# Token sums of a Strassen product on VectorE, three plain column blocks, earlier w_down loads, and an embedding gate without its ScalarE scaling

## The chip, the cores and the metric

The program runs on one core of a Trainium2 chip. The metric is the device time of one execution in microseconds (us), as a median of several executions. The engines' names in the profile are: PE is TensorE (matrix products and transposes), PEld its weight loads, DVE is VectorE, ACT is ScalarE, POOL is GpSimd, and SP is SyncE, which here only issues DMAs. L2209 means line 2209 of the kernel.

## What is computed

The program runs two transformer blocks over 1024 tokens of 1024 channels, all in fp32. The first block (two kinds of attention and a mixture of experts) and the mixer of the second are not touched. What matters is the end of the second block:

```python
h = rms_norm(x, g_ffn_pre[l])
up = h @ w_up[l]                                   # 1024 x 1024 by 1024 x 6144
gate_h = causal_dwconv(up[..., :D_FF], ffn_conv_w[l], ffn_conv_b[l])
hid = jax.nn.gelu(gate_h) * up[..., D_FF:]         # D_FF = 3072
x = x + rms_norm(hid @ w_down[l], g_ffn_post[l])

ple_gate = jax.nn.sigmoid(rms_norm(x, g_ple_gate[l]) @ w_ple_gate[l])
ple = rms_norm(p[l].astype(x.dtype) @ w_ple_proj[l], g_ple_post[l])
x = x + ple_gate * ple
```

## The kernel before

**Products.** Each fp32 operand is split into a high and a low half: the high half is a copy rounded by ScalarE (L86), the low half a subtraction on VectorE (L89; in some stages on POOL). A product is then three matmuls (L341 high by high, L342 low by high, L343 high by low). Tile names end in h and l: `wh`, `wl` are the halves of a weight chunk, `h3h`, `h3l` those of the normalized tokens of the FFN.

**Weight chunks.** A queue serves chunks in the order in which they are needed (`queue`, `pump`, `fetch`, `split_w`). A chunk takes a raw buffer, SP issues its DMA (L196), ACT and DVE split it into a pair of `wh`, `wl` slots, and the raw buffer is free again. A chunk's DMA can't be issued before a raw buffer is free, and SP issues in program order.

**The first FFN product, w_up.** There are `NC` = 24 column blocks, each with a gate half and a value half. The first `plain` = 2 blocks are computed directly: four chunks, each for two halves of 512 tokens, 24 matmuls for each half (192 in all). The order is half 0 of all four chunks first, then half 1, which needs the last token tile (tile 7). The other 22 blocks are Strassen pairs: gate and value chunk together take seven products of 12 matmuls (84 where the plain form takes 96). A pair has four weight parts: `u` and `v` are the loaded chunks, `s` and `d` are sums of them, made on POOL (`wsum`, L238) and split by ACT (L227) and DVE (L228). A block passes through a convolution gate (`fg`: ACT L2185, DVE L2188, gelu on ACT L2191), and DVE multiplies gate and value (L2209 in a plain block). The result is stored to DRAM (L2195) as `hid_d`.

**Token sums.** The Strassen products need sums of the tokens' quadrants, `t1` to `t4` (`fast_operands`, L262 to L304). They are made once, in two parts of 256 columns (`n` = 0, 1), while the plain blocks run. Each part is ten sums of 128x1024 (L272, L273): seven on POOL (`gp`), three on DVE (`dv`), chained through the temporaries `fty`, `ftx1`, `ftx3` and `ftx2`. Three splits give `ft1`, `ft2`, `ft3`; `t4` is split last, after the plain blocks.

Ahead of this stage the last token tiles are normalized: `max` sums on POOL (L2128), squares on ACT, a chain of tiny DVE steps (L401 to L411, tiles `nss`, `nr`, `ans`, `anr`), the scaled tile `nxn` (DVE, L2138), eight transposes on PE (L436, tile `tr`), and the split into `h3h`, `h3l`.

**The second FFN product, w_down** (`ffn_down`). Two halves of the tokens, each 24 steps over k with 24 matmuls, into all eight PSUM banks (tiles `tr`, `mm`). Chunks are the rows of w_down (`down`) and pairs of blocks of `hid_d` (`hid`); they are queued after `ffn_up` returns.

**The tail.** Eight token tiles, each with two column halves of 24 matmuls with `w_ple_gate`. The tokens' transposes `fhT`, `flT` come from `finish_pair`, two tiles at a time: norms, eight transposes of a tile, then ACT (L86) and DVE (L89) split them. Each half goes through a sigmoid (ACT L2416, tile `og`), a product with the embedding (DVE L2417), a sum (POOL L2418) and a DMA (L2419). The embedding `ple` of tile t + 2 is loaded after tile t (SP, L2398), scaled for each token by ACT (L2399) and multiplied by a gain on POOL (L2400); it has two buffers. In the tail ACT's instructions stand in the order in which the code writes them; elsewhere a scheduler orders each engine's instructions.

Of the kernel before, what the change touches and what calls it, by code (L numbers as in the profile page):

```python
# [17 lines left out]
F32 = mybir.dt.float32  # L18
# [49 lines left out]
class Kernel:  # L68
# [193 lines left out]
    def fast_operands(self, pool, tmp):  # L262
# [7 lines left out]
        dv, gp = nc.vector, nc.gpsimd  # L270
        f = lambda x: x.bitcast(F32)
        sub = lambda e, out, x, y: e.tensor_tensor(out, x, y, op=OP.subtract)  # L272
        add = lambda e, out, x, y: e.tensor_tensor(out, x, y, op=OP.add)  # L273
        x2s = [tmp.tile([P, 4, 256], F32, name=f"ftx2{n}") for n in range(2)]
        self.fast = dict(b11=b11, b21=b21, b22=b22, t1=t1, t2=t2, t3=t3, t4=t4)
        for n, x2 in enumerate(x2s):
# [3 lines left out]
            sub(gp, y, f(h12[1]), f(h11[1]))  # L280
            sub(dv, x1, f(h12[0]), f(h11[0]))
            yield 2.5
            add(dv, x1, x1, y)
            sub(gp, x3, f(h22[1]), f(h12[1]))
            yield 2.5
            self.split(*o1, x1)
            sub(gp, y, f(h22[0]), f(h12[0]))
            yield 2.5
            sub(dv, x2, f(h22[0]), x1)
            add(gp, x3, x3, y)  # L290
            yield 2.5
            add(gp, x2, x2, f(h22[1]))
            self.split(*o3, x3)
            yield 2.5
            self.split(*o2, x2)
            sub(gp, x2, f(h21[0]), x2)
            add(gp, x2, x2, f(h21[1]))
            yield 2.5

        def last():  # L300
            for n, x in enumerate(x2s):
                self.split(*(z[:, :, 256 * n:256 * n + 256] for z in t4), x)
# [1868 lines left out]
    def ffn_up(self, pu, up, pairs, es_t):  # L2171
# [55 lines left out]
        for c, (u, s, d, v) in enumerate(pairs, len(up) // 2):  # L2227
            add = lambda e, out, p, q: e.tensor_tensor(out, p, q, op=OP.add)  # L2228
# [40 lines left out]
    def block2(self, es):  # L2269
# [66 lines left out]
        NC, plain = DFF // P, 2  # L2336
# [24 lines left out]
        self.ffn_up(pu, up, pairs, es_t)  # L2361
        for half in range(2):
            for k in range(0, NC, 2):
                self.queue([hid[half][k // 2], *down[half][k:k + 2]])
        self.settle()
        es_u.close()
        es_h.close()
        acc = self.pool(es_x, "accp", side="right").tile([P, NT, D], F32, name="acc")
# [18 lines left out]
        self.add_w(es_x, "plew", 4, only=ch_p)  # L2387
# [5 lines left out]
        pl, embs = fin["pool"], []  # L2393

        def emb(t):
            if t < NT:
                e = pl.tile([P, D], F32, name="ple", tag="ple", bufs=2)
                nc.sync.dma_start(e, self.ple_d[t * P:(t + 1) * P])  # L2398
# [4 lines left out]
        with self.tc.manual_schedule(engines={mybir.EngineType.Activation}):  # L2403
            for t in range(2):
                emb(t)
# [169 lines left out]
```

## Time and profile before

| | |
|---|---|
| median of 3 executions | 3524.74 us (3518.86 to 3526.04) |
| the profiled execution | 3530.14 us, span 3528.4 us, mean granted clock of PE 0.952 |
| busy share of the span | PE 90%, PEld 72%, DVE 66%, ACT 45%, POOL 35% |
| PE, in tenths of 40 slices | `6987799788899799999888999999978999999997` |

The page gives shares of the span, and slices of 88 us each. A row of a timeline gives the start, the duration, the engine and line, what is written from what, and in brackets how long the engine had stood idle and what released it. Matmul durations overlap, since PE works on several at once, so the distance between two starts is what a matmul costs. A row of the windows gives for a stretch the busy time of every engine with the number of its instructions, PE's granted clock and the share of the DMA engines. The waits name the engine and line that stood idle, what it waited for, the sum, the number and the longest.

### The profile page before, as it was taken

To read this page: it belongs to the slowest core of one execution; us is meant where nothing else is said; L and a number is where in the kernel's file an instruction comes from. 1 tells how busy PE (TensorE), PEld (TensorE's weight loads), DVE (VectorE), ACT (ScalarE), POOL (GpSimd) and SP (SyncE) were. 2 spreads that over 40 slices of the span, in tenths; PEclk is the share of its full clock that TensorE was granted. 3 is DMA by queue.
4 is the path that set the end of the run, shared out by engine and by line. 5 is a ranking of instruction groups with operands and counts; after the bars stand their busy time and mean duration, and the time that the engine had idled before them with its cause. 6 is when DMAs were issued, how large, how long until landed. Compare 5 with 4: busy or idle time off the path is not lost. (4 is left out here: it accounts for less than half of the span.)

```text
span 3528.4 us, 40979 instructions
## 1 busy us (share of the span) xinstructions
PE 3170.0 (90%) x14117; PEld 2531.6 (72%) x14117; DVE 2314.9 (66%) x3549; ACT 1604.9 (45%) x2406; POOL 1247.4 (35%) x872
## 2 busy tenths in 40 slices
PE   6987799788899799999888999999978999999997
PEld 4865577567677577777666887888756877778776
DVE  6799954678655799999986554214477566653543
ACT  3553222568633566666566673211233333333332
POOL 2133223455204566666541121000136665520113
PEclk9998899889999799999999999999999999999998
DMA  5211366663454899999875213433341222244431
GB/s 192 62 51 55 109 220 200 152 167 80 150 172 154 300 320 317 316 320 325 292 239 162 67 56 107 135 115 109 119 128 60 82 80 78 78 173 143 163 112 60
DMA packets 365087, 548.42 MB, mean 155 GB/s; under 512 B 33292, under 2 KB 184224, under 8 KB 364876
## 3 DMA queue, kind: packets, MB, share of 16 engines
q1 hardware_dynamic: 343744, 503.53, 43.8%
q0 software_dynamic: 11440, 24.77, 2.7%
q10 hardware_dynamic: 9692, 17.48, 1.5%
q8 instruction: 112, 1.84, 0.2%
q14 instruction: 99, 0.81, 0.1%
HBM read 451.63 MB, written 88.78 MB: 153 GB/s over the span
## 5 line engine op out<-in xcount | busy, mean ns | idle before, releaser
L89 DVE TENSOR_TENSOR wl<-wr,wh 128x1024 fp32r<-128x1024 f32 (+1 forms) x489 | 821.2, 1703 | 473.9 <-ACT wh L86 472.9
L86 ACT ACTIVATE wh<-wr 128x1024 fp32r<-128x1024 f32 (+1 forms) x612 | 624.6, 1037 | 579.2 <-PE mm L342 179.5
L89 POOL TENSOR_TENSOR wl<-wr,wh 128x1024 fp32r<-128x1024 f32 x145 | 385.7, 2702 | 94.8 <-ACT wh L86 88.3
L341 PE MATMUL mm<-h2h,wh 128*128 128x512 f32 x576 | 229.4, 399 | 1.2 <-ACT h2h L86 1.2
L343 PE MATMUL mm<-h2h,wl 128*128 128x512 f32 x576 | 227.3, 395 | 0.0
L342 PE MATMUL mm<-h2l,wh 128*128 128x512 f32 x576 | 227.2, 394 | 0.0
L341 PE MATMUL mm<-wh,hTh 128*128 128x512 f32 (+1 forms) x368 | 145.1, 394 | 39.0 <-POOL wh L88 17.6
L343 PE MATMUL mm<-h3h,wl 128*128 128x512 f32 x416 | 165.2, 398 | 4.4 <-DVE ans L401 2.4
L341 PE MATMUL mm<-h3h,wh 128*128 128x512 f32 x416 | 167.4, 403 | 1.5 <-ACT wh L86 1.2
L342 PE MATMUL mm<-h3l,wh 128*128 128x512 f32 x416 | 165.2, 397 | 0.0
L2128 POOL TENSOR_TENSOR max<-max,antmp 128x512 f32<-128x512 f32 x16 | 25.2, 1600 | 386.3 <-DVE antmp L2127 374.5
L342 PE MATMUL pb<-wl,xgh 128*128 128x512 f32 x256 | 109.7, 429 | 48.5 <-DVE wl L89 47.3
L342 PE MATMUL mm<-wl,hTh 128*128 128x512 f32 (+1 forms) x368 | 142.3, 387 | 5.5 <-POOL wl L89 4.9
L343 PE MATMUL mm<-wh,hTl 128*128 128x512 f32 (+1 forms) x368 | 141.5, 385 | 0.0
L228 DVE TENSOR_TENSOR wl<-wsum,wh 128x1024 fp32r<-128x1024 f32 x44 | 55.4, 1259 | 119.4 <-ACT wh L227 119.4
L1384 POOL TENSOR_SCALAR sm<-sm,src 128x128 f32<-128x128 f32 (+7 forms) x128 | 96.2, 757 | 100.7 <-DVE src L1383 71.8
L341 PEld LDWEIGHTS mm<-h2h,wh 128*128 128x128 f32 x576 | 108.5, 188 | 27.5 <-ACT h2h L86 1.5
L342 PEld LDWEIGHTS mm<-h2l,wh 128*128 128x128 f32 x576 | 108.5, 188 | 26.2 <-issue 1.2
L343 PEld LDWEIGHTS mm<-h2h,wl 128*128 128x128 f32 x576 | 108.4, 188 | 25.2
L341 PE MATMUL mm<-hTh,wh 128*128 128x512 f32 x256 | 106.4, 416 | 19.6 <-POOL wh L88 12.1
L1409 DVE TENSOR_TENSOR ptl<-tr,pth 128x512 fp32r<-128x512 f32 x192 | 102.5, 550 | 26.0 <-ACT pth L1408 24.7
L342 PE MATMUL pa<-wl,xgh 128*128 128x512 f32 x256 | 103.4, 404 | 17.0 <-DVE wl L89 14.0
(667 smaller groups left out, 8909.5 us busy)
## 6 DMA issues: line engine op xcount, KB each, us to landing
wr<-in_exp_w SPq DMA_DIRECT2D x384, 512.0 KB
wr<-in_w_in SPq DMA_DIRECT2D x72, 512.0 KB
wr<-in_w_up SPq DMA_DIRECT2D x48, 512.0 KB
wr<-in_w_down SPq DMA_DIRECT2D x48, 512.0 KB
sg_d<-sg SPq DMA_DIRECT2D x64, 256.0 KB
score<-in_ada_w ACTq DMA_DIRECT2D x32, 512.0 KB
hid_d<-fg SPq DMA_DIRECT2D x24, 512.0 KB
wr<-hid_d SPq DMA_DIRECT2D x24, 512.0 KB
```

The lines of the kernel that those rows point to most:

```text
L86: self.nc.scalar.activation(hi, x, AF.Copy)
L89: (lo_eng or self.nc.vector).tensor_tensor(lo, x, hi.bitcast(F32), op=OP.subtract)
L228: nc.vector.tensor_tensor(lo, f, hi.bitcast(F32), op=OP.subtract)
L341: mm(ps, w[0], x[0], start=first, stop=False)
L342: mm(ps, w[0], x[1], start=False, stop=False)
L343: mm(ps, w[1], x[0], start=False, stop=last)
L1384: nc.gpsimd.tensor_scalar(sm, sm, rc[:, l:l + 1], 1.0, op0=OP.mult, op1=OP.mult)
L1409: self.lag.append(lambda c0=c0, th=th, tl=tl, tr=tr: nc.vector.tensor_tensor(tl[:, c0:], tr[:, c0:], th[:, c0:].bitcast(F32), op=OP.subtract))
L2128: nc.gpsimd.tensor_tensor(x[:, cs], x[:, cs], tmp, op=OP.add)
```

## The change

There are four parts.

- All twenty token sums are on DVE, in another order within a part, and part n = 1, which holds the last token tile, goes first.
- `plain` is 3: one block more is computed directly, and there is one Strassen pair fewer.
- The first six chunks of w_down's stage (`hid` 0, `down` 0, 1, `hid` 1, `down` 2, 3) are queued when the last but one Strassen pair begins (`near_end`), the rest after `ffn_up`; three more raw buffers (`ffz`) exist from then on.
- ACT no longer scales the embedding: the factor goes into DVE's product with `og`, which becomes a scalar_tensor_tensor. The embedding has three buffers, and the first three tiles are loaded and multiplied by the gain ahead of the second half of w_down; `w_ple_gate` gets three slots of its own instead of four.

```diff
--- before.py
+++ after.py
@@ -267,38 +267,38 @@
         b11, b21, b12, b22 = q(0, 0), q(1, 0), q(0, 1), q(1, 1)
         t = [tuple(pool.tile([P, 4, 512], F32R, name=f"ft{i}{x}") for x in "hl") for i in (1, 2, 3)] + [b12]
         t1, t2, t3, t4 = t
-        dv, gp = nc.vector, nc.gpsimd
         f = lambda x: x.bitcast(F32)
-        sub = lambda e, out, x, y: e.tensor_tensor(out, x, y, op=OP.subtract)
-        add = lambda e, out, x, y: e.tensor_tensor(out, x, y, op=OP.add)
-        x2s = [tmp.tile([P, 4, 256], F32, name=f"ftx2{n}") for n in range(2)]
+        sub = lambda out, x, y: nc.vector.tensor_tensor(out, x, y, op=OP.subtract)
+        add = lambda out, x, y: nc.vector.tensor_tensor(out, x, y, op=OP.add)
+        x2s = {n: tmp.tile([P, 4, 256], F32, name=f"ftx2{n}") for n in (1, 0)}
         self.fast = dict(b11=b11, b21=b21, b22=b22, t1=t1, t2=t2, t3=t3, t4=t4)
-        for n, x2 in enumerate(x2s):
+
+        for n, x2 in x2s.items():
             y, x1, x3 = (tmp.tile([P, 4, 256], F32, name=i, tag=i) for i in ("fty", "ftx1", "ftx3"))
             h11, h21, h12, h22, o1, o2, o3 = (tuple(z[:, :, 256 * n:256 * n + 256] for z in x)
                                               for x in (b11, b21, b12, b22, t1, t2, t3))
-            sub(gp, y, f(h12[1]), f(h11[1]))
-            sub(dv, x1, f(h12[0]), f(h11[0]))
+            sub(y, f(h12[1]), f(h11[1]))
+            sub(x1, f(h12[0]), f(h11[0]))
             yield 2.5
-            add(dv, x1, x1, y)
-            sub(gp, x3, f(h22[1]), f(h12[1]))
+            add(x1, x1, y)
+            self.split(*o1, x1)
             yield 2.5
-            self.split(*o1, x1)
-            sub(gp, y, f(h22[0]), f(h12[0]))
+            sub(y, f(h22[1]), f(h12[1]))
+            sub(x3, f(h22[0]), f(h12[0]))
             yield 2.5
-            sub(dv, x2, f(h22[0]), x1)
-            add(gp, x3, x3, y)
+            add(x3, x3, y)
+            sub(x2, f(h22[0]), x1)
             yield 2.5
-            add(gp, x2, x2, f(h22[1]))
             self.split(*o3, x3)
+            add(x2, x2, f(h22[1]))
             yield 2.5
             self.split(*o2, x2)
-            sub(gp, x2, f(h21[0]), x2)
-            add(gp, x2, x2, f(h21[1]))
+            sub(x2, f(h21[0]), x2)
             yield 2.5
+            add(x2, x2, f(h21[1]))
 
         def last():
-            for n, x in enumerate(x2s):
+            for n, x in x2s.items():
                 self.split(*(z[:, :, 256 * n:256 * n + 256] for z in t4), x)
 
         self.fast_last = last
@@ -2168,7 +2168,7 @@
         for i, ch in enumerate(chunks):
             self.dense_n(ch, src, lambda t, ps: emit(t, i % 2, ps), range(4 * (i // 2), 4 * (i // 2) + 4))
 
-    def ffn_up(self, pu, up, pairs, es_t):
+    def ffn_up(self, pu, up, pairs, es_t, near_end):
 
 
         nc = self.nc
@@ -2225,6 +2225,8 @@
             return ps
 
         for c, (u, s, d, v) in enumerate(pairs, len(up) // 2):
+            if c == NC - 2:
+                near_end()
             add = lambda e, out, p, q: e.tensor_tensor(out, p, q, op=OP.add)
             s1, s2, s3, s5 = (pu.tile([P, 512], F32, name=n, tag=n) for n in ("fs1", "fs2", "fs3", "fs5"))
             new(c)
@@ -2333,7 +2335,7 @@
         hp = self.pool(es_h, "hT3")
         self.hT, self.hcount = [hp.tile([P, KT, S], F32R, name=n) for n in ("h3h", "h3l")], 0
         wu, wd = a["w_up_2"][0], a["w_down_2"][0]
-        NC, plain = DFF // P, 2
+        NC, plain = DFF // P, 3
         self.hid_d = self.dram.tile([NC, P, S], F32, name="hid_d")
         blocks = [[blk(wu, i * DFF + c * P) for i in range(2)] for c in range(NC)]
         up = [self.chunk_t(b, KT) for x in blocks[:plain] for b in x]
@@ -2358,13 +2360,13 @@
         self.sums = pu = self.pool(es_u, "ffnu")
         self.later_steps(0.0, self.fast_operands(fp, self.pool(es_t, "fastt")))
         self.add_w(es_f, "ffx", 2, 2, side="right")
-        self.ffn_up(pu, up, pairs, es_t)
-        for half in range(2):
-            for k in range(0, NC, 2):
-                self.queue([hid[half][k // 2], *down[half][k:k + 2]])
+        later = [c for n in range(2) for k in range(0, NC, 2) for c in (hid[n][k // 2], *down[n][k:k + 2])]
+        self.ffn_up(pu, up, pairs, es_t, lambda: self.queue(later[:6]))
         self.settle()
         es_u.close()
         es_h.close()
+        self.add_w(es_x, "ffz", 0, 3, side="right")
+        self.queue(later[6:])
         acc = self.pool(es_x, "accp", side="right").tile([P, NT, D], F32, name="acc")
         self.hcount = 0
         ch_p = [Chunk([(lambda r: r, w.rearrange("(k p) c -> p k c", p=P))], [P, 2, 512])
@@ -2384,25 +2386,24 @@
                 next(fin[p], None)
 
         self.ffn_down(acc, hid[0], down[0], 0, lambda k, i: None)
-        self.add_w(es_x, "plew", 4, only=ch_p)
+        self.add_w(es_x, "plew", 3, only=ch_p)
+        pl, embs = fin["pool"], []
+
+        def emb(t):
+            if t < NT:
+                e = pl.tile([P, D], F32, name="ple", tag="ple", bufs=3)
+                nc.sync.dma_start(e, self.ple_d[t * P:(t + 1) * P])
+                nc.gpsimd.tensor_tensor(e, e, fin["ge"], op=OP.mult)
+                embs.append(e)
+
+        for t in range(3):
+            emb(t)
         self.queue(ch_p)
         todo = {(0, 7): [0], (2, 7): [0], (4, 7): [0, 1], (6, 7): [0, 1], (8, 7): [1],
                 (NC - 1, 4): [0], (NC - 1, 6): [0]}
         self.ffn_down(acc, hid[1], down[1], 1, lambda k, i: step(*todo.get((k, i), ())))
 
-        pl, embs = fin["pool"], []
-
-        def emb(t):
-            if t < NT:
-                e = pl.tile([P, D], F32, name="ple", tag="ple", bufs=2)
-                nc.sync.dma_start(e, self.ple_d[t * P:(t + 1) * P])
-                nc.scalar.activation(e, e, AF.Copy, scale=fin["r"][:, t:t + 1])
-                nc.gpsimd.tensor_tensor(e, e, fin["ge"], op=OP.mult)
-                embs.append(e)
-
         with self.tc.manual_schedule(engines={mybir.EngineType.Activation}):
-            for t in range(2):
-                emb(t)
             step(2)
             for t in range(NT):
                 x, e = fin["x", t], embs.pop(0)
@@ -2414,10 +2415,10 @@
                         self.mm3(ps, (x[0][:, k], x[1][:, k]), (wh[:, k % 2], wl[:, k % 2]), k == 0, k == KT - 1)
                     o = pl.tile([P, 512], F32, name="og", tag="og", bufs=2)
                     nc.scalar.activation(o, ps, AF.Sigmoid)
-                    nc.vector.tensor_tensor(o, o, e[:, cs], op=OP.mult)
+                    nc.vector.scalar_tensor_tensor(o, o, fin["r"][:, t:t + 1], e[:, cs], op0=OP.mult, op1=OP.mult)
                     (nc.vector if t == NT - 1 and c else nc.gpsimd).tensor_tensor(o, o, acc[:, t, cs], op=OP.add)
                     nc.sync.dma_start(self.out[0, t * P:(t + 1) * P, cs], o)
-                emb(t + 2)
+                emb(t + 3)
                 step(*{0: [1, 2], 1: [1, 1, 2], 2: [2, 3, 3], 3: [2, 2, 3], 4: [3], 5: [3, 3]}.get(t, ()))
         for c in ch_p:
             self.free(c)
```

On DVE at the end of the token norms, with token tile 7's split (`h3l<-tr,h3h`) and the sums (`fty`, `ftx`, `ft1l` to `ft3l`). Of before:

```order
L89 TENSOR_TENSOR wl<-wr,wh 128x1024
L402 TENSOR_SCALAR nr<-nss 128x1
L272 TENSOR_TENSOR ftx_21812<-h3h 128x1024
L403 TENSOR_SCALAR nr<-nr 128x1
L273 TENSOR_TENSOR ftx_21812<-ftx_21812,fty 128x1024
L407 TENSOR_SCALAR rst<-nr,nss 128x1
L407 TENSOR_SCALAR rst<-anr,ans 128x1
L411 SCALAR_TENSOR_TENSOR nr<-rst,nr 128x1
L272 TENSOR_TENSOR ftx_21809<-h3h,ftx_21812 128x1024
```

Here DVE's three sums of the first part stand between the tiny steps of the token norms (`nr`, `anr`). Of the change, from tile 7's scaled form on:

```order
L2138 SCALAR_TENSOR_TENSOR nxn<-max,nr,maf 128x1024
L2209 TENSOR_TENSOR fg<-mm,fg 128x512
L89 TENSOR_TENSOR h3l<-tr,h3h 128x4x128 x2
L271 TENSOR_TENSOR fty<-h3l 128x1024
L271 TENSOR_TENSOR ftx_21812<-h3h 128x1024
L271 TENSOR_TENSOR ftx_21813<-h3h 128x1024
L272 TENSOR_TENSOR ftx_21812<-ftx_21812,fty 128x1024
L271 TENSOR_TENSOR fty<-h3l 128x1024
L89 TENSOR_TENSOR ft1l<-ftx_21812,ft1h 128x4x256
```

No sum stands ahead of tile 7's split any more, and the first sum reads its `h3l`. Further on in the same run of rows, up to the weights of the third plain block:

```order
L89 TENSOR_TENSOR ft1l<-ftx_21919,ft1h 128x4x256
L272 TENSOR_TENSOR ftx_21920<-ftx_21920,fty 128x1024
L271 TENSOR_TENSOR ftx_21810<-h3h,ftx_21919 128x1024
L89 TENSOR_TENSOR wl<-wr,wh 128x1024
L2188 SCALAR_TENSOR_TENSOR fg<-fu_21798,colsc,fg 128x512
L89 TENSOR_TENSOR ft3l<-ftx_21920,ft3h 128x4x256
L2188 SCALAR_TENSOR_TENSOR fg<-fu_21798,colsc,fg 128x512
L272 TENSOR_TENSOR ftx_21810<-ftx_21810,h3l 128x1024
L89 TENSOR_TENSOR wl<-wr,wh 128x1024
```

Behind tile 7's split there are 21 sums and splits, and then, as the 22nd, the low half `wl` of the fifth plain chunk. The sixth chunk's `wl` is the 27th, the first pair's `u` the 30th. On POOL, the piece of the difference between the `max` sums of the token norms and the first pair's weight sums (the `x4` and `x2` rows of `max` become one row of eight):

```order
-L2128 TENSOR_TENSOR max<-max,antmp 128x512 x2
-L272 TENSOR_TENSOR fty<-h3l 128x1024
-L272 TENSOR_TENSOR ftx_21920<-h3l 128x1024
-L272 TENSOR_TENSOR ftx_21809<-h3h,ftx_21809 128x1024
-L273 TENSOR_TENSOR ftx_21809<-ftx_21809,h3l 128x1024
-L272 TENSOR_TENSOR fty<-h3h 128x1024
-L273 TENSOR_TENSOR ftx_21920<-ftx_21920,fty 128x1024
-L273 TENSOR_TENSOR ftx_21810<-ftx_21810,h3l 128x1024
-L272 TENSOR_TENSOR ftx_21810<-h3h,ftx_21810 128x1024
-L273 TENSOR_TENSOR ftx_21810<-ftx_21810,h3l 128x1024
```

POOL goes straight from the norms to the weight sums. On SP, the DMAs around the end of the Strassen pairs, before:

```order
L2195 DMA hid_d<-fg 128x1024
L196 DMA wr<-in_w_down 128x1024
L196 DMA wr<-hid_d 128x2x512
L2195 DMA hid_d<-fg 128x1024
L196 DMA wr<-hid_d 128x2x512
L196 DMA wr<-in_w_down 128x1024
L2195 DMA hid_d<-fg 128x1024
L196 DMA wr<-in_w_down 128x1024 x2
```

and of the change:

```order
L196 DMA wr<-in_w_up 128x8x128 x2
L2195 DMA hid_d<-fg 128x1024
L196 DMA wr<-hid_d 128x2x512
L196 DMA wr<-in_w_down 128x1024
L2195 DMA hid_d<-fg 128x1024
L196 DMA wr<-in_w_down 128x1024
L196 DMA wr<-hid_d 128x2x512
L196 DMA wr<-in_w_down 128x1024 x2
L2195 DMA hid_d<-fg 128x1024
```

Between the same three stores stood four chunks of w_down's stage, and now stand six, `hid` 0, `down` 0 and 1, `hid` 1, `down` 2 and 3, in the order in which they are used. On ACT in the tail, where a group of four `fhT` is the split of one tile's transposes, before:

```order
L2416 ACTIVATE og<-mm 128x512 x2
L2399 ACTIVATE ple<-ple,pler 128x1024
L86 ACTIVATE fhT<-tr 128x512 x4
L2437 ACTIVATE fj,fss<-acc 128x1024 x2
L2416 ACTIVATE og<-mm 128x512 x2
L2399 ACTIVATE ple<-ple,pler 128x1024
```

and of the change:

```order
L2417 ACTIVATE og<-mm 128x512 x4
L86 ACTIVATE fhT<-tr 128x512 x4
L2438 ACTIVATE fj,fss<-acc 128x1024 x2
L2417 ACTIVATE og<-mm 128x512 x2
L2438 ACTIVATE fj,fss<-acc 128x1024 x2
```

The split `fhT` stands directly behind the sigmoids; the scaling between them is gone.

## Rows read from the trace of the kernel before

**Rows 1.** Windows: stretch, its length, busy us (instructions) by engine, PE's clock, DMA, GB/s.

```profile
2595.00:2712.00 117.00, 82.82 (x334) 63.80 (x333) 100.01 (x127) 40.21 (x59) 75.94 (x38) 0.90 0.28 85
2712.00:3112.00 400.00, 399.95 (x1701) 317.38 (x1700) 244.97 (x285) 146.31 (x203) 235.39 (x160) 1.00 0.25 80
3121.00:3144.00 23.00, 18.38 (x67) 14.18 (x66) 11.43 (x21) 6.52 (x7) 3.40 (x3) 0.85 0.72 254
3395.00:3529.00 134.00, 104.59 (x459) 84.11 (x456) 50.79 (x91) 36.17 (x60) 46.38 (x25) 0.90 0.19 63
```

**Rows 2.** PE's timeline, from token tile 6's transposes to the second Strassen pair.

```profile
2638.31 1.94 PE L436 MATMUL tr<-ident,nxn 128*128 128x128 f32 x8 [10.71 <-DVE anr L411]
...
2648.75 0.80 PE L341 MATMUL mm<-h3h,wh 128*128 128x512 f32 x1 [0.25 <-ACT h3h L86]
...
2667.12 0.40 PE L341 MATMUL mm<-h3h,wh 128*128 128x512 f32 x1
2667.35 0.39 PE L342 MATMUL mm<-h3l,wh 128*128 128x512 f32 x1
...
2696.40 0.77 PE L341 MATMUL mm<-ft3h,wh 128*128 128x512 f32 x1 [8.12 <-DVE fg L2209]
...
2712.00 0.39 PE L341 MATMUL mm<-ft1h,wh 128*128 128x512 f32 x1
```

**Rows 3.** DVE's timeline over the token norms and the first sums.

```profile
2619.81 3.13 DVE L89 TENSOR_TENSOR wl<-wr,wh 128x1024 fp32r<-128x1024 f32 x1
...
2622.93 3.35 DVE L272 TENSOR_TENSOR ftx<-h3h 128x1024 f32<-128x1024 f32 x1
...
2626.39 2.13 DVE L273 TENSOR_TENSOR ftx<-ftx,fty 128x1024 f32<-128x1024 f32 x1
...
2628.81 2.21 DVE L411 SCALAR_TENSOR_TENSOR nr<-rst,nr 128x1 f32<-128x1 f32 x1
2630.94 1.21 DVE L272 TENSOR_TENSOR ftx<-h3h,ftx 128x1024 f32<-128x1024 f32 x1
...
2632.26 2.10 DVE L411 SCALAR_TENSOR_TENSOR anr<-rst,anr 128x1 f32<-128x1 f32 x1
2634.29 0.15 DVE L411 SCALAR_TENSOR_TENSOR nr<-rst,nr 128x1 f32<-128x1 f32 x1
...
2634.78 1.89 DVE L411 SCALAR_TENSOR_TENSOR anr<-rst,anr 128x1 f32<-128x1 f32 x1
...
2652.95 1.21 DVE L89 TENSOR_TENSOR ft3l<-ftx,ft3h 128x1024 fp32r<-128x1024 f32 x1
2654.09 1.21 DVE L89 TENSOR_TENSOR ft2l<-ftx,ft2h 128x1024 fp32r<-128x1024 f32 x1
```

**Rows 4.** POOL's timeline: a token sum, the first `d` sum of weights.

```profile
2660.98 3.26 POOL L273 TENSOR_TENSOR ftx<-ftx,h3l 128x1024 f32<-128x1024 f32 x1
...
2683.49 3.42 POOL L238 TENSOR_TENSOR wsum<-wr 128x512 f32<-128x512 f32 x2
```

**Rows 5.** PE's timeline at the start of w_down.

```profile
3121.36 0.39 PE L341 MATMUL tr<-wh 128*128 128x512 f32 x1
...
3137.50 1.65 PE L341 MATMUL tr<-wh 128*128 128x512 f32 x3 [4.11 <-ACT wh L86]
...
3139.37 0.63 PE L342 MATMUL tr<-wl,wh 128*128 128x512 f32 x1
3139.80 0.63 PE L343 MATMUL tr<-wh,wl 128*128 128x512 f32 x1
```

**Rows 6.** ACT's timeline at the start of w_down.

```profile
3136.39 2.00 ACT L86 ACTIVATE wh<-wr 128x1024 fp32r<-128x1024 f32 x2 [6.14 <-DMA wr<-in_w_down]
```

**Rows 7.** Waits of all engines in the tail: sum, number, longest.

```profile
ACT ple L2399 <- DMA ple<-ple_d: 36.1, 6, 9.4
...
PE mm L341 <- ACT fhT L86: 23.3, 3, 10.5
...
ACT og L2416 <- POOL og L2418: 6.7, 2, 4.4
```
## The prediction

> **What bounds the kernel now.** I read the page's slices first (PE at 7 or less in a few slices late in the program), then windows over the three places that the change touches, then the timelines there. In the Strassen pairs PE is full: 399.95 of 400 us, clock 1.00 [rows 1], so nothing can be won between 2712 and 3112 except by fewer matmuls. Three stretches are not full. From 2595 to 2712, where the token norms end, the plain blocks run and the sums are made, PE is busy 82.82 of 117 us. From 3121 to 3144, where w_down begins, it is busy 18.38 of 23. In the tail it is busy 104.59 of 134. In each the clock is below full (0.90, 0.85, 0.90). The gaps are 34.2, 4.6 and 29.4 us. A matmul costs 0.2325 us at full clock (2667.12 to 2667.35 in [rows 2]) and 0.43 at the lower level of 1.2 GHz (3139.37 to 3139.80 in [rows 5]).
>
> **A: the token sums and the third plain block.** PE's two long stalls are 10.71 us ahead of token tile 6's transposes and 8.12 us ahead of the first product on `ft3` [rows 2]. Both end on DVE. The reader is to see in [rows 3] why DVE is late: the same form of sum takes 3.35 us at 2622.93 and 1.21 at 2630.94, and a tiny L411 step takes 2.21, 2.10 and 1.89 where its like takes 0.15. The slow ones lie beside POOL's token sums, of which one takes 3.26 [rows 4].
>
> *Removed from the norm chain.* DVE's three sums between the tiny steps took 3.35 + 2.13 + 1.21 = 6.7 us; in the new order they stand behind tile 7. With POOL idle the three slow steps lose 6.20 - 0.45 = 5.8, and the `wl` at 2619.81 takes 1.21 in place of 3.13 (1.9). That is 14.4; I take 13.9, since hand-overs between engines stay. Tile 7's own chain holds no sum and keeps its length. So the first matmul of the second token half moves from 2648.75 [rows 2] to 2634.9.
>
> *Added behind it.* PE then has 96 matmuls on the four loaded chunks (22.3 us, to 2657.2), while DVE does tile 7's split and 21 sums and splits ahead of the fifth chunk's `wl`. Their pitch without POOL is 1.14 us (2652.95 to 2654.09 in [rows 3]): 23 x 1.14 = 26.2, so that `wl` ends at 2661.1. PE waits 2 to 4 us there, partly covered by matmuls that need only `wh`; with the slow clock behind it I take 3.6. The sixth chunk's `wl` comes five operations (6 us) later, under 10.7 us of matmuls on the fifth.
>
> *The weight sums.* In before the first `d` sum starts on POOL at 2683.49 [rows 4], because the token sums stand ahead of it. Now POOL has nothing else; the sum waits for the second raw chunk alone, and I place it near 2675, ahead of PE's use at about 2694. So the 8.12 us stall goes.
>
> *Sum.* From 2634.9: 96 + 96 plain matmuls (the third block included) and 84 of the first pair, 276 x 0.2325 = 64.2, plus 3.6, give 2702.7 for the start of the second pair, with four blocks done. In before the second pair starts 24 matmuls ahead of 2712.00 [rows 2], at 2706.4, with three blocks done; a pair takes (3121.36 - 2706.4) / 21 = 19.76 us [rows 2, 5], so four are done at 2726.2. The gain is 23.5; the third plain block's 12 extra matmuls (2.8 us) are inside it. I take 22, since one small stall I can't see is likely. Bounds: 12, if only the earlier tile 7 is won and a stall of some 10 us grows at the new `wl` waits; 26, if the fifth chunk is in time and the clock holds.
>
> **B: the start of w_down.** PE stops for 4.11 us at 3137.50 [rows 5], waiting for ACT's `wh`, which itself waited 6.14 us for a w_down chunk's DMA [rows 6]: the chunks pass one by one through a raw buffer. In the new order six chunks in order of use stand among the last stores, enough for 96 matmuls (22 us), and the extra buffers serve the next. The stall's 4.1 us go, and of the clock's loss in this window (0.15 of 23 us is 3.5 [rows 1]) the part that falls on matmuls, some 2.4: 6.5 together. Bounds: 0, if those buffers come no earlier than the old ones; 7.6, all of it. I am near the upper end because the waiting engine's row names the DMA, and the order moves just that. The small wait for a PSUM bank ahead of it stays.
>
> **C: inside w_down.** PE is the bound; three loads of `ple` and the POOL gain products beside it are hidden. Without POOL's cover the price would be a delayed `wl` of at most a sum's 3 us: bound 0 to 3 lost, taken at 0.
>
> **D: the tail.** The largest wait that PE meets is for `fhT` on ACT: 23.3 us in 3 times, the longest 10.5 [rows 7]. In the old order ACT's scaling of `ple` stands ahead of the split, and it waits 36.1 us in 6 times for its DMA, the longest 9.4. Take that away and ACT reaches the split right after the sigmoid. Two ACT instructions (36.17 / 60 = 0.6 us each [rows 1]) stay at each of the three transitions at most: between 0 and 3.6 us, so 19.7 to 23.3 are won; I take 21, and 1 more for matmuls that ran at the lower clock behind the three stalls (the window's clock of 0.90 would allow several). D is 22. What the scaling did moves into DVE's product; DVE is busy 50.79 of 134 us, so a slightly longer form costs nothing. What is late next is POOL: it now waits for the same DMA in its own queue, with the sums of `og` behind it, and SP's output DMAs behind those. But the tile loaded there is needed three tiles later, not two, and nobody on PE waits for an `og` sum until both `og` buffers are held. Bounds: 14, if a wait of POOL's kind returns in part; 27, with the clock.
>
> **Sum.** 22 + 6.5 + 22 = 50.5. The profiled execution took 3530.1 us, which would be 3479.6; it lay 5.4 above the median of the runs, so against the median I say **3474**. All three at their low ends (12 + 0 + 14 = 26) give 3499, all at their high ends (26 + 7.6 + 27 = 61) 3464; executions scatter by about 4 below.
>
> **Rivals.**
>
> *1. DVE becomes the bound of stretch A.* DVE is busy 100.01 of 117 us there, POOL 75.94 [rows 1]; fourteen sums more at 1.14 are 16 us, 116 of 117. If the 100 us were work that stays, the stretch could not become shorter, A would give nothing, and the time would be 3474 + 22 = 3496. Against it: much of the 100 us is not work, as the long and short rows of one form show (six rows of [rows 3] carry some 11 us of it). For it: the new sums all stand ahead of weights that PE wants. Chance 0.10. The Trainium skill's page Perfetto Trace Analysis, sections Identifying the Most-Contended Engine and Optimizing Scalar/DVE Operations, calls the engine with the highest occupancy the one to relieve, and advises handing work away from a saturated DVE, which speaks against this part; it adds that a move between GpSimd and DVE might not help, as they share a read port. By it the time is this rival's; the trace sides with the second half of the sentence more than the first, for the sums do slow each other.
>
> *2. POOL's wait takes ACT's place in the tail.* ACT already waits for POOL's `og` sums, 6.7 us in 2 times, the longest 4.4 [rows 7]. If such a wait stood ahead of each of the three splits, 3 x 4.4 = 13 us would return, less the 2 that I left there: 11, and 3485. For it: POOL works in order and its product now waits for the DMA. Against it: the third buffer. Chance 0.14.
>
> *3. The sums stay slow on DVE, and the weights queue behind them: slower.* If each of the 27 operations up to the sixth chunk's `wl` took the 3.35 us of the contended row instead of 1.14, they would end 90 us after 2634.9, at 2725; PE, with 96 matmuls and 46 of the fifth chunk (33 us) to do meanwhile, would stand some 57 us instead of my 3.6. That costs 54, as much as all three gains: 3474 + 54 = 3528. It decides from about 3.25 us an operation; below that the change is still faster. Against it: POOL has no sums left to contend with except weight sums that wait for raw chunks. Chance 0.04. The Trainium skill's page SBUF — State Buffer, section Who interferes with whom, states that a DVE instruction with two SBUF inputs contends with a GpSimd instruction that reads SBUF, and that the one shuts the other out for its whole length; by that only those few sums that meet one of POOL's are long, and the trace agrees so far, with 3.35 us beside POOL and 1.21 without.
>
> *4. The early queue does not load earlier.* If the six chunks find no free raw buffer until the last pair is done, B is 0: 3480.5. For it: the pair's two raw chunks hold buffers to its end. Against it: before, too, loads four chunks of this stage between the last stores. Chance 0.06.
>
> **How the numbers follow.** The forecast has 0.66. It and rivals 1, 2 and 4 lie between 3474 and 3496; with the bounds and the scatter of the terms I give 3460 to 3495, which leaves out rival 3, part of rival 1 and the forecast's own far ends, under 0.2 together. A measurement of this kernel tells about 0.2% (7 us) from no change. Faster by more than that: 0.95. Rival 3 lies at 3528 and spreads to both sides of 3532: within 0.2% 0.03, slower 0.02.
>
> **What would show it.** Right: no PE stall of 10 us at tile 6's transposes and none of 8 at the first `ft3` product; DVE's sums at about 1.2 us each; a short PE wait at the fifth plain chunk; 20 pairs that start near 2703; no wait for `wh` at the start of w_down; waits for `fhT` under 1.5 us each, in a tail of about 112 us instead of 134. Wrong: sums on DVE of 2 us and more, a new stall of PE at the plain chunks, PE waiting for `fhT` behind an `og` that waits for POOL, or a new stall in w_down beside POOL's gain products.

## The result and the profile after

The changed kernel takes 3471.48 us (median of 4, 3468.52 to 3474.49), the kernel before in the same comparison 3525.39 (3518.86 to 3528.51). The ratio is 0.9849, with a 95% interval of 0.9832 to 0.9867: 53.9 us faster. The forecast was 3474, between 3460 and 3495.

Ahead of the change the two programs are the same, and still their profiled executions differ there: token tile 4's transposes start at 2604.33 in before and at 2599.75 in after. So I count every stage from that point. From there to the last matmul before takes 918.3 us and after 863.3, 55.0 less. The page of after, its first part and PE's slices:

```profile
PE 3161.7 (91%) x14129; PEld 2522.5 (73%) x14129; DVE 2298.2 (66%) x3557; ACT 1595.0 (46%) x2396; POOL 1198.3 (35%) x850
...
PE   6997799788899789888888999999988999999998
```

The windows of after that answer to [rows 1]; the first is moved by the lead of some 4.6 us, the second lies within the pairs, the third and fourth begin as far ahead of their stage's first matmul as there:

```profile
2590.41:2707.41 117.00, 104.35 (x449) 81.80 (x448) 96.73 (x153) 47.91 (x68) 32.91 (x24) 0.99 0.33 99
2683.00:3083.00 400.00, 399.94 (x1698) 316.52 (x1698) 240.37 (x280) 144.79 (x199) 234.27 (x159) 1.00 0.25 82
3093.13:3116.13 23.00, 23.00 (x101) 18.45 (x100) 13.66 (x22) 6.80 (x8) 4.07 (x3) 1.00 0.84 296
3360.27:3468.90 108.63, 99.56 (x459) 80.05 (x456) 60.28 (x92) 30.64 (x55) 46.17 (x24) 0.99 0.23 73
```

In all three stretches the gap and the lower clock went together. In the first DVE did 14 sums more and was busy 96.73 us in place of 100.01. The start of w_down has no gap left. The tail is 25 us shorter with the same 459 matmuls.

PE's timeline of after, which answers to [rows 2, 5]:

```profile
2619.91 1.06 PE L436 MATMUL tr<-ident,nxn 128*128 128x128 f32 x8
...
2629.03 1.06 PE L436 MATMUL tr<-ident,nxn 128*128 128x128 f32 x8 [2.23 <-DVE nxn L2138]
...
2656.84 0.50 PE L343 MATMUL mm<-h3h,wl 128*128 128x512 f32 x1 [0.93 <-DVE wl L89]
...
2703.08 0.40 PE L341 MATMUL mm<-ft1h,wh 128*128 128x512 f32 x1
...
3093.49 0.40 PE L341 MATMUL tr<-wh 128*128 128x512 f32 x1
```

Tile 6's transposes start with no wait (before: 10.71), tile 7's wait 2.23 (before: 3.84), the fifth plain chunk's wait is 0.93, and no product on `ft3` waits. Every sum on DVE is now short (the source line of the first sums: engine, form, count, duration in ns as least, median, most):

```profile
L271 DVE TENSOR_TENSOR ftx<-h3h x4: 1218/1218/1220, 2632.7 to 2645.3; 128x1024 f32<-128x1024 f32 x4
```

and POOL comes to the first `d` sum of weights with idle time ahead of it:

```profile
2670.80 3.04 POOL L238 TENSOR_TENSOR wsum<-wr 128x512 f32<-128x512 f32 x2 [5.89 <-DVE wl L228]
```

By stages, from tile 4's transposes on (the difference of the first starts of each stage):

| stage | before | after | gain |
|---|---|---|---|
| A: to the first matmul of w_down | 517.0 | 493.7 | 23.3 |
| B, C: w_down, to the first matmul on `fhT` | 277.8 | 271.0 | 6.8 |
| D: the tail, to the last matmul | 123.4 | 98.6 | 24.8 |

In the tail no wait for `fhT` is left. The waits of PE and the longest of POOL for a DMA there:

```profile
PE tr L436 <- DVE flT L89: 3.5, 2, 2.8
...
POOL ple L2396 <- DMA ple<-ple_d: 15.1, 5, 4.2
```

### The profile page after: what moved, and what is told of

It reads as the page before. It is cut to its first block, busy times and chain, and to the rows that moved or that the text cites. A ratio compares the mean times of both kernels' runs of the same rounds, so it can differ in the third digit from the quotient of the medians.

```text
span 3468.9 us, 40965 instructions
## 1 busy us (share of the span) xinstructions
PE 3161.7 (91%) x14129; PEld 2522.5 (73%) x14129; DVE 2298.2 (66%) x3557; ACT 1595.0 (46%) x2396; POOL 1198.3 (35%) x850
## 5 line engine op out<-in xcount | busy, mean ns | idle before, releaser
L238 POOL TENSOR_TENSOR wsum<-wr 128x512 f32<-128x512 f32 x63 | 90.8, 1455 | 104.0 <-DVE wl L228 54.5
```

The source lines that it names most:

```text
L238: gp = lambda i, x, y, op: nc.gpsimd.tensor_tensor(f[:, i], x, y, op=op)
```

## The experiments

Eleven versions of the changed kernel; each diff is against it, and "..." stands for lines left out. A stage is read from one profiled execution of a version, a median from four to six executions, and the two can differ by up to 9 us. How far a stage scatters shows where versions run the same program in it: stage A took 493.4 to 495.6 us in nine traces, w_down 270.8 to 271.1 in four, the tail 98.0 to 100.8 in seven. So the stages and the waits in them decide, and the median is given beside them.

### The token sums back on POOL

All of `fast_operands` as before:

```diff
-        for n, x2 in x2s.items():
+        for n, x2 in enumerate(x2s):
...
-            sub(y, f(h12[1]), f(h11[1]))
-            sub(x1, f(h12[0]), f(h11[0]))
+            sub(gp, y, f(h12[1]), f(h11[1]))
+            sub(dv, x1, f(h12[0]), f(h11[0]))
...
```

> The changed kernel, with the token sums put back as they were: fourteen on POOL, six on DVE, part 0 first. The third plain block, the early queue and the tail stay. My theory: the gain of stretch A came from DVE no longer being slowed beside POOL ahead of tiles 6 and 7. Then DVE's sum of 3.3 us is back, PE stalls again for about 10 us at tile 6 and 4 at tile 7, and the time is 3471.5 + 13.8 + 1 = 3486 us. The 8 us stall at the first ft3 product should stay away, since the third plain block gives POOL 22 us more. Rival, the third plain block alone won stretch A: 3472.

Measured: 3488.73 us (ratio to before 0.9903, 0.9887 to 0.9920), and the stages are 17.1 us longer. PE waits again in the two old places (10.71 and 3.84 us in before), and for new reasons in the first pairs:

```profile
2629.27 1.94 PE L436 MATMUL tr<-ident,nxn 128*128 128x128 f32 x8 [7.37 <-DVE anr L411]
...
2638.46 1.94 PE L436 MATMUL tr<-ident,nxn 128*128 128x128 f32 x8 [3.40 <-DVE nxn L2138]
...
2713.85 0.50 PE L341 MATMUL mm<-ft1h,wh 128*128 128x512 f32 x1 [1.69 <-DVE fs L2230]
```

The second half of the tokens starts 13.4 us later than in the changed kernel, and the first pairs lose another 3.5 in three waits of 0.8 to 1.7. The 8 us stall did not return, so the third block does cover POOL, as expected. Next, this run's DVE rows:

```profile
2611.67 3.11 DVE L89 TENSOR_TENSOR wl<-wr,wh 128x1024 fp32r<-128x1024 f32 x1
...
2614.77 3.32 DVE L272 TENSOR_TENSOR ftx<-h3h 128x1024 f32<-128x1024 f32 x1
...
2619.70 2.28 DVE L411 SCALAR_TENSOR_TENSOR nr<-rst,nr 128x1 f32<-128x1 f32 x1
...
2623.04 0.26 DVE L407 TENSOR_SCALAR rst<-nr,nss 128x1 f32<-128x1 f32 x1
2623.22 2.10 DVE L411 SCALAR_TENSOR_TENSOR anr<-rst,anr 128x1 f32<-128x1 f32 x1
...
2625.73 1.89 DVE L411 SCALAR_TENSOR_TENSOR anr<-rst,anr 128x1 f32<-128x1 f32 x1
```

and POOL's at the same time:

```profile
2613.66 3.34 POOL L272 TENSOR_TENSOR ftx<-h3l 128x1024 f32<-128x1024 f32 x1
2619.56 2.40 POOL L272 TENSOR_TENSOR fty<-h3h 128x1024 f32<-128x1024 f32 x1 [2.56 <-DVE ftx L273]
2622.04 3.27 POOL L273 TENSOR_TENSOR ftx<-ftx,fty 128x1024 f32<-128x1024 f32 x1
2625.27 2.33 POOL L273 TENSOR_TENSOR ftx<-ftx,h3l 128x1024 f32<-128x1024 f32 x1
```

Add the durations. The three long L411 steps on one element per partition end at 2621.98, 2625.32 and 2627.62; POOL's sums end at 2621.96, 2625.31 and 2627.60. Each ends with POOL's instruction, as if it had stood still until then. DVE's sum at 2614.77 ends 1.1 us, its own length, after POOL's at 2617.00. The L407 step at 2623.04, which has one tensor input, takes 0.26 while POOL works. This is the rule that the prediction cited from the Trainium skill, SBUF — State Buffer, Who interferes with whom; this trace agrees, for the whole length of an instruction.

Not all of the 13.4 us is standing still. Up to tile 6 the rows of DVE beside POOL are 9.8 us longer than their likes (5.8 in the three L411 steps, 2.1 in the sum, 1.9 in a `wl` of 3.11 us). The rest is about what the three sums themselves take at 1.14 us each, which this version puts back ahead of tile 6. The order of the parts is tried alone further on.

### Two plain blocks

```diff
-        NC, plain = DFF // P, 3
+        NC, plain = DFF // P, 2
```

> The changed kernel with two plain blocks in place of three, so 12 matmuls less (2.8 us) and one Strassen pair more. My theory: the third block covers the sums on DVE; without it PE waits behind the sums at the first pair, for the s weights and the ft2 and ft3 operands, 3 to 9 us in all, so 3472 to 3478, most likely 3474. Rival, the cover is not needed: 3471.5 - 2.8 = 3468.7 or less.

Measured: 3474.91 (0.9863, 0.9846 to 0.9879); the stages are 7.7 us longer in its profile. The 2.8 us of matmuls that it saves are more than spent, above all by waits from the first pair's `u` on:

```profile
2646.95 0.61 PE L343 MATMUL mm<-h3h,wl 128*128 128x512 f32 x1 [2.42 <-DVE wl L89]
...
2661.46 0.50 PE L341 MATMUL mm<-ft3h,wh 128*128 128x512 f32 x1 [2.14 <-ACT wh L227]
...
2692.54 0.50 PE L341 MATMUL mm<-h3h,wh 128*128 128x512 f32 x1 [0.96 <-DVE fs L2230]
```

Seven such waits sum to 7.7 us. So the third plain block pays as cover for DVE's sums. Its median is only 3.4 us above that of the changed kernel, which the scatter can hide; the waits can't be argued away.

### Part 0 of the sums first

```diff
-        x2s = {n: tmp.tile([P, 4, 256], F32, name=f"ftx2{n}") for n in (1, 0)}
+        x2s = {n: tmp.tile([P, 4, 256], F32, name=f"ftx2{n}") for n in (0, 1)}
```

> The changed kernel with all sums on DVE, but part 0 first, which does not need token tile 7. The order then puts five sums of 1.14 us among the small steps ahead of tile 6's scaled form, and others ahead of tile 7's. My theory: both tiles are later by about 6 us, and the 0.9 us wait at the fifth chunk goes: 3477. Rival, with POOL quiet the order of the parts does not matter: 3471.

Measured: 3473.36 (0.9855, 0.9831 to 0.9880). Half of this was a miss. The lateness came: PE waits 10.35 us for tile 7's scaled form, and the second token half starts 7.2 us later than in the changed kernel.

```profile
2634.60 1.94 PE L436 MATMUL tr<-ident,nxn 128*128 128x128 f32 x8 [10.35 <-DVE nxn L2138]
```

But 3.9 us came back by the end of the pairs: 2.2 from more pairs at the quicker of two pitches (the last section says where these come from), the rest from the plain blocks, where PE no longer waits at the fifth chunk. The stages are 2.5 us longer, little more than their scatter; whether the order of the parts matters to the whole time stays open.

### No early queue and no extra buffers; each alone

```diff
-        self.ffn_up(pu, up, pairs, es_t, lambda: self.queue(later[:6]))
+        self.ffn_up(pu, up, pairs, es_t, lambda: None)
...
-        self.add_w(es_x, "ffz", 0, 3, side="right")
-        self.queue(later[6:])
+        self.queue(later)
```

> The changed kernel with all chunks of the w_down stage queued after the last Strassen pair again, and without the three extra raw buffers. My theory: the 4 us stall on ACT's wh early in w_down and the slow clock behind it are back: 3471.5 + 6.5 = 3478. Rival, the early queue loads nothing earlier: 3471.5, and the stall of before would be gone for another reason.

Only the buffers taken away:

```diff
-        self.add_w(es_x, "ffz", 0, 3, side="right")
```

> The changed kernel with the early queue of six chunks, but without the three extra raw buffers. My theory: the order in which the first six chunks take the buffers is what cures the start of w_down; PE is the bound after it, so the extra buffers give nothing: 3471 to 3473, and 271 us from the first matmul of w_down to the first on fhT, as in the changed kernel. Rival, the extra buffers do it: 279 us there and 3478.

Only the early queue taken away:

```diff
-        self.ffn_up(pu, up, pairs, es_t, lambda: self.queue(later[:6]))
+        self.ffn_up(pu, up, pairs, es_t, lambda: None)
...
-        self.queue(later[6:])
+        self.queue(later)
```

> The changed kernel with the three extra raw buffers, but with all chunks queued after the last pair. My theory: the first chunks still pass one by one through one early buffer, because the extra ones exist only once the last pair is done, so the stall of 4 to 5 us on ACT's wh comes back: 277 to 279 us from the first matmul of w_down to the first on fhT, 3477. Rival, the extra buffers do it: 271 us and 3472.

| | median us | ratio to before | w_down, to the first matmul on `fhT` |
|---|---|---|---|
| changed kernel | 3471.48 | 0.9849 (0.9832 to 0.9867) | 271.0 |
| neither | 3478.58 | 0.9870 (0.9854 to 0.9887) | 279.4 |
| early queue alone | 3467.40 | 0.9838 (0.9824 to 0.9852) | 270.8 |
| extra buffers alone | 3472.22 | 0.9851 (0.9834 to 0.9868) | 276.7 |

PE's waits at the start of w_down with neither (rows of its timeline):

```profile
3109.00 1.65 PE L341 MATMUL tr<-wh 128*128 128x512 f32 x3 [4.70 <-ACT wh L86]
...
3122.96 0.50 PE L341 MATMUL tr<-wh 128*128 128x512 f32 x1 [1.35 <-ACT wh L86]
```

and the one with the extra buffers alone:

```profile
3109.64 1.65 PE L341 MATMUL tr<-wh 128*128 128x512 f32 x3 [4.76 <-ACT wh L86]
```

The early queue does it, the buffers spare at most the second, smaller wait and are worth nothing beside the queue. The waits show this, the medians don't: the median with the extra buffers alone, 3472.22, is where I had put the rival, though its profiled execution, the one with the stall, took 3477.18. The median of the early queue alone lies below the 3471 to 3473 that I expected, and the intervals of the two ratios overlap.

The reason differs a little from what I had written. The late queue loads as many chunks early. Of the version with neither, first SP's issues, then ACT's splits:

```profile
3048.37 0.37 SPq L196 DMA_DIRECT2D wr<-hid_d  x1
3056.37 0.35 SPq L196 DMA_DIRECT2D wr<-in_w_down  x1
3068.21 0.33 SPq L196 DMA_DIRECT2D wr<-in_w_down  x1
3075.29 0.37 SPq L196 DMA_DIRECT2D wr<-hid_d  x1
3084.04 7.30 SPq L196 DMA_DIRECT2D wr<-in_w_down  x2
...
3081.49 1.05 ACT L86 ACTIVATE wh<-wr 128x1024 fp32r<-128x1024 f32 x1
3088.66 1.06 ACT L86 ACTIVATE wh<-wr 128x1024 fp32r<-128x1024 f32 x1 [2.53 <-DMA wr<-in_w_down]
3094.17 1.06 ACT L86 ACTIVATE wh<-wr 128x1024 fp32r<-128x1024 f32 x1 [4.46 <-DMA wr<-in_w_down]
```

Four chunks are on their way by 3075.29, as in the changed kernel by 3077.22, but ACT splits one and must then wait for two w_down chunks that SP issues only from 3084.04 on. In the changed kernel its splits up to 3096.01 wait for no load. So the early buffers went to chunks that are not the first in use (which ones, the traces don't name), and what the early queue mends is who gets the early buffers.

### The tail: scaling and buffers apart

The tail of before (scaling on ACT, two buffers, the loads of the first two tiles at the start of the tail):

```diff
-        for t in range(3):
-            emb(t)
...
-                e = pl.tile([P, D], F32, name="ple", tag="ple", bufs=3)
+                e = pl.tile([P, D], F32, name="ple", tag="ple", bufs=2)
...
+                nc.scalar.activation(e, e, AF.Copy, scale=fin["r"][:, t:t + 1])
...
+            for t in range(2):
+                emb(t)
...
-                    nc.vector.scalar_tensor_tensor(o, o, fin["r"][:, t:t + 1], e[:, cs], op0=OP.mult, op1=OP.mult)
+                    nc.vector.tensor_tensor(o, o, e[:, cs], op=OP.mult)
...
-                emb(t + 3)
+                emb(t + 2)
```

> The changed kernel with the tail of before: ACT scales the embedding, two buffers, the loads of the first two tiles in the tail. My theory: three waits of PE for fhT, some 23 us in all, are back, and the clock's loss behind them: the stretch from the first matmul on fhT to the last, 98.6 us in the changed kernel, becomes about 123, and the time 3471.5 + 24 = 3495. Rival, the wait only changes its place: 3472 to 3483.

Scaling on ACT, but three buffers and early loads:

```diff
+                nc.scalar.activation(e, e, AF.Copy, scale=fin["r"][:, t:t + 1])
                 nc.gpsimd.tensor_tensor(e, e, fin["ge"], op=OP.mult)
...
-                    nc.vector.scalar_tensor_tensor(o, o, fin["r"][:, t:t + 1], e[:, cs], op0=OP.mult, op1=OP.mult)
+                    nc.vector.tensor_tensor(o, o, e[:, cs], op=OP.mult)
```

> The changed kernel with ACT's scaling put back, but with the three buffers and the early loads kept. My theory: what counts is that ACT, in its fixed order, waits for a DMA that SP can issue only behind the tile's output; the third buffer doesn't change that. So the waits for fhT are back as in the kernel with the whole tail put back: 3491 to 3495. Rival, the third buffer and the early loads are what cured it: 3472 to 3475.

No scaling on ACT, two buffers and no early loads:

```diff
-        for t in range(3):
-            emb(t)
...
-                e = pl.tile([P, D], F32, name="ple", tag="ple", bufs=3)
+                e = pl.tile([P, D], F32, name="ple", tag="ple", bufs=2)
...
+            for t in range(2):
+                emb(t)
...
-                emb(t + 3)
+                emb(t + 2)
```

> The changed kernel without ACT's scaling, but with two buffers and the loads in the tail as before. My theory: POOL waits for the DMA off PE's path, so the gain is there without the third buffer: 3471 to 3474. Rival, POOL's late gain product holds the sums and the og buffers, and ACT's sigmoids stand ahead of fhT: 3480 to 3490.

| scaling on ACT | buffers, first loads | median us | ratio to before | tail us |
|---|---|---|---|---|
| no | 3, early | 3471.48 | 0.9849 (0.9832 to 0.9867) | 98.6 |
| no | 2, in the tail | 3468.75 | 0.9848 (0.9830 to 0.9866) | 99.4 |
| yes | 3, early | 3487.21 | 0.9896 (0.9880 to 0.9911) | 119.2 |
| yes | 2, in the tail | 3495.60 | 0.9920 (0.9904 to 0.9936) | 125.9 |

By the tails the scaling on ACT costs 26.5 us with two buffers and 20.6 with three. By the medians it is 26.9 and 15.7; the profiled execution with scaling and three buffers took 3496.84, the longest of its six. The third buffer and the early loads (not tried apart) give nothing without the scaling. With it they spare one of three waits, since one load of six comes early: a gain of 6.7 us in the tail where I had expected none, and a median below the 3491 to 3495 that I had put down. The waits of the tail with scaling and three buffers (with two, PE waits 26.0 us in 3 times):

```profile
ACT ple L2396 <- DMA ple<-ple_d: 34.5, 5, 9.7
...
PE mm L341 <- ACT fhT L86: 19.4, 2, 10.7
```

Without scaling and with two buffers POOL waits for that DMA instead, and PE has no wait for `fhT`:

```profile
POOL ple L2401 <- DMA ple<-ple_d: 16.3, 5, 4.7
```

### The residual sums of the tail on DVE

After the change PE's only waits in the tail are for `flT`, 3.5 us in 2 times. DVE's rows of the changed kernel ahead of the longer one show two `og` products that take 5.63 us:

```profile
3410.65 5.63 DVE L2418 SCALAR_TENSOR_TENSOR og<-og,pler,ple 128x512 f32<-128x512 f32 x2
3416.20 1.87 DVE L89 TENSOR_TENSOR flT<-tr,fhT 128x512 fp32r<-128x512 f32 x3
```

and POOL's rows show its two residual sums at the same time, as with the token sums:

```profile
3409.66 6.07 POOL L2451 TENSOR_TENSOR acc<-acc,fx 128x1024 f32<-128x1024 f32 x2 [1.21 <-issue]
```

```diff
-            nc.gpsimd.tensor_tensor(acc[:, t], acc[:, t], xt[j], op=OP.add)
+            nc.vector.tensor_tensor(acc[:, t], acc[:, t], xt[j], op=OP.add)
```

> The changed kernel with the residual sum of the last norms (acc + fx, eight of 128x1024, about 3.05 us each on POOL) on DVE. The one PE wait of the tail that is left, 2.8 us for flT at 3416.9, stands behind two og products that take 5.6 us beside those sums. My theory: the sums take 1.2 us each on DVE, the products 0.7 again, the wait goes, and the tail is 2 to 4 us shorter: 3468 to 3470. Rival, DVE has no room there and flT waits behind the sums: 3471.5 or more.

Measured: 3464.16 (0.9830, 0.9812 to 0.9849). The tail takes 96.3 us, and w_down 268.8 in place of 271.0, where a 1.86 us wait for a `wl` beside such a sum is gone too. By the stages this is 4 us, the upper end of what I had expected; the median lies 7.3 us below the changed kernel's, more than the traces explain. DVE does sums and products in less time than the products alone took:

```profile
3411.43 2.35 DVE L2451 TENSOR_TENSOR acc<-acc,fx 128x1024 f32<-128x1024 f32 x2
3413.70 1.41 DVE L2418 SCALAR_TENSOR_TENSOR og<-og,pler,ple 128x512 f32<-128x512 f32 x2
```

### Residual sums on DVE and no extra buffers

```diff
-        self.add_w(es_x, "ffz", 0, 3, side="right")
...
-            nc.gpsimd.tensor_tensor(acc[:, t], acc[:, t], xt[j], op=OP.add)
+            nc.vector.tensor_tensor(acc[:, t], acc[:, t], xt[j], op=OP.add)
```

> The changed kernel without the three extra raw buffers and with the residual sums of the last norms on DVE: the two edits of earlier runs together. If they add up, the stretch from token tile 4's transposes to the last matmul is 859 us, where the changed kernel has 863, with the tail at 96 in place of 98.6 and the 1.9 us wait inside w_down gone; the time 3464 to 3468. Rival, DVE is now too full in the tail and the og products or flT come late: 3470 or more.

Measured: 3463.78 (0.9823, 0.9810 to 0.9837); 858.8 us from tile 4's transposes to the last matmul, against 863.3. By the stages it beats both kernels. By the median it is 7.7 us below the changed kernel's, though they were timed in different comparisons.

## Why the prediction was right

**A, 22 forecast, 23.3 measured.** The first matmul of the second token half came 13.8 us earlier (18.4 less the 4.6 of lead), where the chain gave 13.9; putting the sums back cost 13.4 there. DVE's pitch of 1.14 us held. The first `d` sum came where it was expected (2670.80 and the lead make 2675.4, against 2675), though its row waits for DVE's `wl` of the part before it and not for a raw chunk.

At the fifth chunk the forecast had 3.6 us, for a wait and the slow clock behind it. The trace has a wait of 0.93 and full clock behind it, but that is the chance of this execution. Of nine versions traced that run the same program here, four wait 0.93 to 0.99 us and five 2.40 to 2.42. The one with neither early queue nor extra buffers waits 2.41. Windows from the first matmul of the second half to the end of that wait, and the 5 us behind it, of the changed kernel and then of that version:

```profile
2630.34:2656.84 26.50, 25.57 (x102) 20.21 (x102) 26.47 (x25) 10.89 (x13) 0.00 (x0) 0.94 0.00 1
2656.84:2661.84 5.00, 5.00 (x21) 4.06 (x22) 5.00 (x6) 1.70 (x2) 1.04 (x1) 1.00 0.37 105
...
2628.32:2654.75 26.43, 24.02 (x103) 19.12 (x103) 26.39 (x25) 11.00 (x13) 0.00 (x0) 1.00 0.00 1
2654.75:2659.75 5.00, 5.00 (x15) 4.02 (x16) 5.00 (x6) 1.69 (x2) 1.07 (x1) 0.66 0.36 105
```

The `wl` comes 26.4 to 26.5 us behind the first matmul in both. In the first PE lost time ahead of it, at a clock of 0.94, and so had less to wait; in the second it waited longer and lost time behind it, at 0.66. From the first matmul of the second half to the second pair's first product on `t1` the forecast gives 73.4 us (64.2 + 3.6, and 24 matmuls); the changed kernel took 72.7 and the other 74.2. So the 3.6 was about right, as a sum of wait and clock.

**B, 6.5 forecast, 6.8 measured** for w_down as a whole. The stall and the slow clock went as said. What carried it was the six chunks *in order of use*; the extra buffers did nothing. Some luck is in the number. The wait of 0.51 us for a PSUM bank, which I had said would stay, is gone too (with neither queue nor buffers it is 1.30), and inside w_down the wait for a `wl` shrank from 2.44 to 1.86. With the stall's 4.11 that is 5.2 us of waits, which leaves 1.6 for the clock, where I had 2.4.

**D, 22 forecast, 24.8 measured.** The waits for `fhT` went whole (23.3 to none); 3.5 us of another wait stay. I allowed 1 us for the clock; the waits alone account for 19.8, so some 5 came with the clock, which went from 0.90 to 0.99. That term was mis-sized.

**The sum**, 50.5 forecast, 53.9 in the medians and 55.0 by stages.

**The rivals.** 1 (DVE becomes the bound) fell: in the stretch DVE was busy 96.73 us with 14 sums more. It had a point, though: from 2640 to 2680 DVE had no time to spare, and PE's 0.93 us wait lies there:

```profile
2640.00:2680.00 40.00, 39.07 (x168) 31.25 (x167) 39.83 (x37) 17.89 (x23) 8.69 (x5) 1.00 0.21 66
```

The advice cited from the Trainium skill's page Perfetto Trace Analysis, Optimizing Scalar/DVE Operations, to hand work away from a saturated DVE, would have pointed away from this change. Its warning about the shared read port is the part that the traces bear out: a sum took 3.32 us beside POOL's and 1.22 after.

2 (POOL's wait in the tail) was seen, POOL waiting 15.1 us for the DMA in 5 times, and it did not reach PE. What was late next I had not named: `flT` on DVE, behind products slowed by POOL. 3 fell, with all sums at 1.22 us. 4 fell: w_down starts with no wait for `wh`.

## What to carry to other kernels

A row on DVE that takes three times as long as its like is a reason to look at POOL's rows of the same time: work moved from POOL to DVE can make DVE less busy. In an engine whose order is fixed, an instruction that waits for a DMA must not stand ahead of one that the bound engine needs; moving it to an engine with slack was worth more than another buffer (26.5 us against 6.7). A block done the plain way is cheap cover where operands are still being made.

## What was not expected

Up to tile 4's transposes the thirteen programs traced compute the same, yet in the traces these start anywhere between 2588.7 and 2604.3 us. That is more than most effects here, and only stages counted from a common point told them apart.

The Strassen pairs run at two pitches. In the changed kernel the first two intervals from one pair's first product on `t1` to the next are 19.57 and 19.53 us, most of the later ones about 19.84; in before the four after the first are about 19.55. With part 0 first, nine of the twenty are at the shorter. Within a long one two or three matmuls start 0.3 to 0.4 us after the one ahead in place of 0.23, and PE's rows show no wait. DVE's rows show what it is. Five PSUM banks (`mm`) take the products in turn, so a pair's second product needs the bank that the product on `t2` of the pair before had, and DVE's sum L2230 empties it. Sum and product, first in a long interval, then in a short one:

```profile
2778.43 0.68 DVE L2230 TENSOR_TENSOR fs<-fs,mm 128x512 f32<-128x512 f32 x1
2779.15 0.50 PE L341 MATMUL mm<-h3h,wh 128*128 128x512 f32 x1
...
2718.91 0.68 DVE L2230 TENSOR_TENSOR fs<-fs,mm 128x512 f32<-128x512 f32 x1
2719.82 0.39 PE L341 MATMUL mm<-h3h,wh 128*128 128x512 f32 x1
```

In the long one the product starts some 0.05 us after the sum's end, in the short one 0.23. It is 0.05 to 0.06 in seventeen of the changed kernel's eighteen longer intervals (all but the last), and in before the sum's lead over PE shrinks from pair to pair (1.07, 0.79, 0.51, 0.27 us) until it is used up. So PE, busy 399.94 of 400 us there, is held a little by DVE in most pairs: the row of a matmul lasts longer than the distance to the next start and covers so short a wait. That nothing can be won there except by fewer matmuls was too strong, by up to 0.3 us a pair. It fits that PE made up time with part 0 first, where DVE's lead in the first pair was 2.3 us in place of 0.43. What sets DVE's own pace wasn't tried; over twenty pairs the two pitches can move a run by up to 6 us.
